# A hybrid decoder block on one core: the residual stream turned at wider steps, retention scores and the 1/rms spread placed later

## The chip, the cores and the metric

The kernel runs on one core of one Trainium2 chip. The metric is the time of one execution on the device in microseconds; the median of three runs of the kernel before is 2200.8 us (2198.17 to 2201.48). Engines are called by their names in the profile: PE multiplies matrices, ACT and DVE work on elements, SP issues the transfers, POOL does next to nothing here.

## What is computed

One decoder block, batch 1, 256 tokens, model width 2048, all in float32:

```python
h = x
h = h + 0.5 * swiglu(rms_norm(h, g1), w_gate1, w_up1, w_down1)        # d_ff 5632
n = rms_norm(h, g_mix)
rq, rk, rv, rg, sq, sk, sv = split(n @ w_in)
ret = retention(rope(rq), rope(rk), rv)       # 8 heads of 128, chunks of 128 tokens
#   s = (q k^T / sqrt(dk)) * decay mask, per head and chunk; intra = s v; state carried from chunk 0 to 1
ret = silu(rg) * group_norm(ret)
swa = sliding_window_attention(rope(sq), rope(sk), sv, sinks)
h = h + concat(ret, swa) @ w_out
h = h + memory_cross_attention(rms_norm(h), rms_norm(mem))
h = h + 0.5 * swiglu(rms_norm(h, g2), w_gate2, w_up2, w_down2)
return rms_norm(h, g_final)
```

## The kernel before

**Products.** Every float32 factor is split in two halves, a high one (a copy to the matmul format) and a low one (what that copy left out), and every product is three matmuls (L470, L471, L472): high by high, low weight by high, high weight by low. The weights are streamed. The unit of the stream is called a step: one piece of 128 x 1024 weights, which ACT copies to `wh` (L71), DVE subtracts to `wl` (L76), and PE uses in twelve matmuls of 128 x 512. A load (L203, 1 MB, on SP's queue) brings two steps. There are three load buffers `wf`, four buffers each of `wh` and `wl`; the halves are made three steps ahead of their matmuls.

**Turning.** Activations are made in one layout (tokens or features across the 128 partitions) and needed in the other. `cross` (L434 to L460) turns one tile pair: two DVE transposes of 32 x 32 blocks into two `t2k` tiles (L444), one step later two writes of 256 KB to a DRAM `box` (L449), two steps later eight reads of 64 KB back (L456), five steps after the start the caller's continuation, which copies or splits what came. All of this goes through the same SP queue as the weight loads, and SP's instructions run in the order in which the program was written.

**Order.** `later(n, task)` puts a task n steps on; `run_due` runs due tasks at the step boundaries between the matmuls. A task's instructions are ordered behind the ones already written on PE, ACT and DVE, so the delay numbers set the place of each task on all engines. PSUM has four temporary tiles `tmp` for such tasks and two accumulators `acc`; `t2k` has ten tiles.

**The three places.**
- The second feed-forward (FFN2) goes through pairs of gate and up units. A pair is 16 steps: eight of gate, after which ACT applies Silu (L507), and eight of up, after which DVE multiplies (L514) and `cross` turns the product. `begin_ffn2` also makes the four 512-column tiles of `h` be turned to the layout of the output (`turn_h`), which the down product at the end of FFN2 needs; this is a `cross` per tile, due 6, 10, 14 and 18 steps on.
- `rqk_done` turns and rotates a group of four retention heads' q and k (DVE L729 to L733) into `qk`; `ret_scores` then makes, per head, two matmuls into one `tmp` tile (L742, L743) and two masked DVE multiplications out of it (L746, L747). There are two groups, g = 0 and g = 1; the scores are due 2 and 3 steps on.
- `Norm.spread` makes 1/rms, which stands per token down the partitions, into rows along the free axis: two DVE broadcasts (L417), two PE transposes (L418), one copy to `rows`. `spread_over` (L425) reads it some 70 us later.

Of the kernel before, what the change touches and what calls it, by code (L numbers as in the profile page):

```python
# [11 lines left out]
F32 = mybir.dt.float32  # L12
F32R = mybir.dt.float32r
AF = mybir.ActivationFunctionType
ALU = mybir.AluOpType
AX = mybir.AxisListType

P = 128
S = 256
# [20 lines left out]
def decoder_block(ctx: ExitStack, tc: tile.TileContext, a: dict, out: bass.AP):  # L40
    nc = tc.nc
# [3 lines left out]
    work = ctx.enter_context(tc.tile_pool(name="work", bufs=1))  # L45
# [7 lines left out]
    def nm(s):  # L53
        uid[0] += 1
        return f"{s}_{uid[0]}"

    def blk(dt=F32R):

        return work.tile([P, 4, 2, S], dt, tag="blk", name=nm("blk"), bufs=13)

    def t2k(dt=F32):
        return work.tile([P, 512], dt, tag="t2k", name=nm("t2k"), bufs=10)

    def tmp_ps(dt=F32):
        return ps_tmp.tile([P, 512], dt, tag="tmp", name=nm("tmp"))
# [4 lines left out]
    def copy(dst, src, **kw):  # L70
        return nc.scalar.activation(dst, src, AF.Copy, **kw)  # L71
# [8 lines left out]
    ident = const.tile([P, P], F32, tag="ident", name="ident")  # L80
# [10 lines left out]
    ones = const.tile([P, P], F32, tag="ones", name="ones")  # L91
# [13 lines left out]
    def later(delay, fn):  # L105
        tasks.append((clock[0] + delay, len(tasks), fn))
# [251 lines left out]
    class Norm:  # L358
# [52 lines left out]

        def spread(self):

            tp = tmp_ps()
            for t in range(2):
                rep = t2k()[:, :P]
                nc.vector.tensor_scalar(rep, ones, self.rs[:, t : t + 1], None, ALU.mult)  # L417
                nc.tensor.transpose(tp[:, t * P : (t + 1) * P], rep, ident)  # L418
            self.rows = work.tile([P, S], F32, tag="rows", name=nm("rows"), bufs=1)
            copy(self.rows, tp[:, :S])  # L420

        def scale(self, t):
            return self.rs[:, t : t + 1]
# [7 lines left out]
    def squares_of(x):  # L431
        return x if len(x.shape) == 4 else x.rearrange("p (q g j) -> p q g j", q=4, g=4)

    def cross(src, then, room=None, delay=TURN):  # L434

        room = [None, None] if room is None else room
        boxes = []  # L440
        out = []
        sq = [t2k() for _ in src]
        for x, v in zip(sq, src):
            nc.vector.transpose(x.rearrange("p (g q j) -> p q g j", g=4, q=4), squares_of(v))  # L444

        def write():
            for x in sq:
                boxes.append(dram.tile([P, 512], F32, tag="box", name=nm("box")))
                nc.sync.dma_start(boxes[-1], x)  # L449

        def read():
            for box, dst in zip(boxes, room):
                dst = t2k() if dst is None else dst
                far = box.rearrange("(i r) (g n) -> g r i n", i=4, g=4)
                for g in range(4):
                    nc.sync.dma_start(dst[32 * g : 32 * g + 32, :].rearrange("p (i n) -> p i n", i=4), far[g])  # L456
                out.append(dst.rearrange("p (i q j) -> p q i j", i=4, q=4))
        later(1, write)
        later(2, read)
        later(delay, lambda: then(out))  # L460
# [252 lines left out]
    def rqk_done(g, which):  # L713
        def done(acc):
            def finish(out):
                if "rot" not in st:
                    st["rot"] = ctab[:, C_COSR : C_COSR + 512].rearrange("p (c s) -> p c s", c=2)
                    nmix.spread_over(st["rot"])
                if which == 0:
                    st["qk"] = blk(F32)  # L720
                qk = st["qk"]
                for t in range(2):
                    x = out[t]
                    cos, sin = (
                        st["rot"][:, c, t * P : (t + 1) * P].rearrange("p (o a j) -> p o a j", o=1, a=4)
                        .broadcast_to([P, 4, 4, 32]) for c in range(2)
                    )
                    r = squares_of(t2k())
                    nc.vector.tensor_tensor(r[:64], x[64:], sin[64:], ALU.mult)  # L729
                    nc.vector.tensor_tensor(r[64:], x[:64], sin[:64], ALU.mult)  # L730
                    nc.vector.tensor_tensor(x, x, cos, ALU.mult)
                    dst = qk[:, :, which, t * P : (t + 1) * P].rearrange("p q (a j) -> p q a j", a=4)
                    nc.vector.tensor_tensor(dst, x, r, ALU.add)  # L733
                if which == 1:
                    for i in range(4):
                        later(2 + i // 2, lambda i=i: ret_scores(g, i, qk))
            cross([acc[:, t, :] for t in range(2)], finish)
        return done

    def ret_scores(g, i, qk):  # L740
        ps = tmp_ps()
        nc.tensor.matmul(ps[:, :S], qk[:, i, 1, :P], qk[:, i, 0, :], start=True, stop=True)  # L742
        nc.tensor.matmul(ps[:, S : S + P], qk[:, i, 1, P:], qk[:, i, 0, P:], start=True, stop=True)  # L743
        sT = t2k()
        dm = st["dmat"][:, g * 4 + i, :]
        nc.vector.tensor_tensor(sT[:, :S], ps[:, :S], dm, ALU.mult)  # L746
        nc.vector.tensor_tensor(sT[:, S : S + P], ps[:, S : S + P], dm[:, :P], ALU.mult)  # L747
        st["sT", g, i] = sT
# [181 lines left out]

    n2 = Norm(G_FFN2, "n2", 4)
    to_h(a["xa_wo"], xo, 1.0, range(4), n2, lambda b: begin_ffn2(b))
    units[-3].then, units[-4].then = None, units[-3]

# [7 lines left out]
    def turn_h(b):  # L942
        if b == 0:
            h.extend(blk(F32).rearrange("p k c s -> p (k c s)") for _ in range(2))

        def made(out):
            for t in range(2):
                copy(squares_of(h[t][:, b * 512 : (b + 1) * 512]), out[t])
        cross([hT[b][:, :, t * P : (t + 1) * P].rearrange("p q (a j) -> p q a j", a=4) for t in range(2)], made)
# [52 lines left out]
    def begin_ffn2(b):  # L1002
        if b == 3:
            for b in range(4):
                later(6 + 4 * b, lambda b=b: turn_h(b))

    ffn(n2, a["ffn2_w_gate"], a["ffn2_w_up"], ffn2_down)
    run_stream()
# [83 lines left out]
```

## Time and profile before

| | before |
|---|---|
| median of three runs | 2200.8 us |
| profiled execution, its own time | 2198.31 us |
| span of its trace | 2196.5 us |
| PE busy | 2175.0 us (99%) |
| DVE busy | 1291.7 us (59%) |
| ACT busy | 1027.5 us (47%) |
| mean granted PE clock | 0.998 |
| moved by DMA | 472.04 MB, 215 GB/s |

The profile comes from one execution. The time of that execution is 1.8 us longer than its span, and 2.5 us under the median. PE is the engine that sets the time; a difference can only come from the moments in which PE waits or runs at a lower clock, and these are few. So the rows to look for are PE's waits, the stretches in which PE's busy time falls short, and what the engine named as releaser was doing itself.

### The profile page before, as it was taken

Reading aid. Unit: us, or ns where it says so; the run is one execution under the profiler, and the core shown is the slowest. Engines: PE = TensorE matmul, PEld = TensorE weight load, DVE = VectorE, ACT = ScalarE, POOL = GpSimd, SP = SyncE. Lnnn points to the kernel's source line nnn. Section 1 sums busy time; section 2 is a strip of 40 time slices with the busy share of each in tenths; the row PEclk is TensorE's granted clock in tenths of the full one; section 3 lists DMA queues with packets and bytes.
Section 4 is the critical chain, followed back from the end, with each engine's and each line's share of the span. In section 5 each row is a group of like instructions: output and inputs, shape, how many; then the busy total and the mean of one; then the engine's idle time right before and its main releaser. Section 6 shows DMA issues by size and latency. Waiting matters only on the chain.

```text
span 2196.5 us, 25627 instructions
## 1 busy us (share of the span) xinstructions
PE 2175.0 (99%) x9844; PEld 1804.2 (82%) x9844; DVE 1291.7 (59%) x1536; ACT 1027.5 (47%) x1258; POOL 10.4 (0%) x17
## 2 busy tenths in 40 slices
PE   9999999999999999999999999999899999999998
PEld 7888888888888888888888888887788888888886
DVE  6555555455556778886775555575555544555554
ACT  6444444444445554544564544454444433444443
POOL 0000000000000000000000000000000000000000
PEclk9999999999999999999999999999999999999999
DMA  7766677667667555556867654676766655666663
GB/s 269 233 217 211 216 228 232 215 214 234 206 222 262 201 185 191 174 191 207 270 232 245 215 174 171 210 250 214 246 214 215 226 196 195 215 207 220 216 215 144
DMA packets 187451, 472.04 MB, mean 215 GB/s; under 512 B 15552, under 2 KB 71616, under 8 KB 187200
## 3 DMA queue, kind: packets, MB, share of 16 engines
q1 hardware_dynamic: 187040, 470.22, 63.7%
q8 instruction: 77, 1.26, 0.2%
q14 instruction: 46, 0.38, 0.1%
q10 hardware_dynamic: 288, 0.18, 0.0%
HBM read 439.93 MB, written 30.41 MB: 214 GB/s over the span
## 4 chain that ended last, share of the span: by engine, by line
PE 95%; DVE 2%; DMA 1%; issue 1%; ACT 0%; SPq 0%; ACTq 0%; POOLq 0%; POOL 0%; DVEq 0%
PE acc L471 31%; PE acc L472 31%; PE acc L470 31%; DMA wf<-in_ffn_w_up 1%; DVE wl L76 1%; PE tmp L471 0%; PE tmp L472 0%; PE tmp L470 0%; ACT wh L71 0%; PE tmp L646 0%; DMA t2k<-box 0%; PE tmp L620 0%; DVE t2k L730 0%; DVE t2k L444 0%; PE tmp L742 0%
## 5 line engine op out<-in xcount | busy, mean ns | idle before, releaser
L76 DVE TENSOR_TENSOR wl<-wf,wh 128x1024 fp32r<-128x1024 f32 (+1 forms) x776 | 942.8, 1217 | 810.0 <-ACT wh L71 803.0
L71 ACT ACTIVATE wh<-wf 128x1024 fp32r<-128x1024 f32 (+1 forms) x776 | 817.4, 1056 | 1014.1 <-PE acc L472 955.9
L470 PE MATMUL acc<-wh,blk 128*128 128x512 f32 (+1 forms) x3104 | 1208.1, 389 | 4.4 <-ACT wh L71 3.2
L471 PE MATMUL acc<-wl,blk 128*128 128x512 f32 (+1 forms) x3104 | 1206.4, 389 | 4.7 <-DVE wl L76 4.6
L472 PE MATMUL acc<-wh,blk 128*128 128x512 f32 (+1 forms) x3104 | 1205.9, 388 | 0.0
L471 PEld LDWEIGHTS acc<-wl,blk 128*128 128x128 f32 x3104 | 583.3, 188 | 125.4 <-DVE wl L76 6.8
L470 PEld LDWEIGHTS acc<-wh,blk 128*128 128x128 f32 x3104 | 583.3, 188 | 124.4 <-ACT wh L71 3.6
L472 PEld LDWEIGHTS acc<-wh,blk 128*128 128x128 f32 x3104 | 583.1, 188 | 120.7 <-DVE blk L356 0.4
L444 DVE STREAM_TRANSPOSE t2k<-t2k 128x512 f32<-128x512 f32 x76 | 49.4, 687 | 16.8 <-ACT t2k L71 16.8
L71 ACT ACTIVATE blk<-t2k 128x512 fp32r<-128x512 f32 (+2 forms) x74 | 44.8, 608 | 9.2 <-DMA t2k<-box 7.3
L76 DVE TENSOR_TENSOR blk<-t2k,blk 128x512 fp32r<-128x512 f32 (+1 forms) x66 | 44.2, 672 | 0.0
L507 ACT ACTIVATE t2k<-acc,n 128x512 f32<-128x512 f32 x44 | 27.9, 686 | 31.6 <-PE acc L472 31.5
L514 DVE SCALAR_TENSOR_TENSOR t2k<-acc,n,t2k 128x512 f32<-128x512 f32 x44 | 31.0, 746 | 15.6 <-PE acc L472 15.6
L71 ACT ACTIVATE blk<-tmp 128x512 fp32r<-128x512 f32 (+2 forms) x53 | 23.9, 459 | 27.5 <-DVE blk L76 19.0
L71 ACT ACTIVATE blk<-h,gains 128x256 fp32r<-128x256 f32 x64 | 27.3, 496 | 5.7 <-DVE h L481 5.7
L356 DVE SCALAR_TENSOR_TENSOR blk<-h,gains,blk 128x256 fp32r<-128x256 f32 x64 | 26.9, 479 | 1.7 <-ACT blk L71 1.7
L393 DVE TENSOR_TENSOR t2k<-t2k,t2k 128x512 f32<-128x512 f32 x35 | 24.0, 685 | 2.3 <-ACT t2k L389 1.0
L76 DVE TENSOR_TENSOR blk<-tmp,blk 64x256 fp32r<-64x256 f32 (+2 forms) x45 | 22.2, 494 | 4.8 <-ACT blk L71 4.5
L471 PE MATMUL tmp<-blk,blk 128*128 128x256 f32 (+1 forms) x80 | 22.6, 282 | 0.6 <-DVE blk L76 0.6
L472 PE MATMUL tmp<-blk,blk 128*128 128x256 f32 (+1 forms) x80 | 22.5, 282 | 0.0
L470 PE MATMUL tmp<-blk,blk 128*128 128x256 f32 (+1 forms) x80 | 22.5, 281 | 0.0
L481 DVE TENSOR_TENSOR h<-h,t2k 128x512 f32<-128x512 f32 x32 | 21.0, 684 | 0.0
(122 smaller groups left out, 433.0 us busy)
## 6 DMA issues: line engine op xcount, KB each, us to landing
wf<-in_ffn_w_down SPq DMA_DIRECT2D x88, 1024.0 KB, 4.9
wf<-in_ffn_w_gate SPq DMA_DIRECT2D x87, 1024.0 KB, 5.1
wf<-in_ffn_w_up SPq DMA_DIRECT2D x87, 1024.0 KB, 5.2
box<-t2k SPq DMA_DIRECT2D x108, 256.0 KB, 2.1
t2k<-box SPq DMA_DIRECT2D x432, 64.0 KB, 4.7
wf<-in_w_in_rqk SPq DMA_DIRECT2D x16, 1024.0 KB, 5.1
wf<-in_w_in_rvg SPq DMA_DIRECT2D x16, 1024.0 KB, 5.0
wf<-in_w_out SPq DMA_DIRECT2D x16, 1024.0 KB, 5.1
```

Of the source, the lines that this page charges most:

```text
L71: return nc.scalar.activation(dst, src, AF.Copy, **kw)
L76: nc.vector.tensor_tensor(lo, src, hi, ALU.subtract)
L356: nc.vector.scalar_tensor_tensor(x[:, k, 1, :], v[:, k, :], g, x[:, k, 0, :], ALU.mult, ALU.subtract)
L393: nc.vector.tensor_tensor(self.sums, self.sums, y, ALU.add)
L444: nc.vector.transpose(x.rearrange("p (g q j) -> p q g j", g=4, q=4), squares_of(v))
L470: nc.tensor.matmul(o, ah, bh, start=start, stop=False)
L471: nc.tensor.matmul(o, ah, bl, start=False, stop=False)
L472: nc.tensor.matmul(o, al, bh, start=False, stop=stop)
L481: nc.vector.tensor_tensor(v, v, out[t], ALU.add)
L507: nc.scalar.activation(gated[b][t], acc[:, t, :], AF.Silu, scale=norm.scale(t))
L514: nc.vector.scalar_tensor_tensor(s[t], acc[:, t, :], norm.scale(t), s[t], ALU.mult, ALU.mult)
```

## The change

Three edits, with no instruction added or left out on PE, DVE, ACT or SP:

1. `begin_ffn2`: the four turnings of `h` are due 19, 35, 51 and 67 steps on instead of 6, 10, 14 and 18.
2. `rqk_done`: the four score tasks are due 4, 4, 5, 5 steps on instead of 2, 2, 3, 3.
3. `Norm.spread`: the two DVE broadcasts go into one `t2k` tile; the PE transposes and the copy are a task of their own, due two steps later.

```diff
         def spread(self):
 
-            tp = tmp_ps()
+            rep = t2k()[:, :S]
             for t in range(2):
-                rep = t2k()[:, :P]
-                nc.vector.tensor_scalar(rep, ones, self.rs[:, t : t + 1], None, ALU.mult)
-                nc.tensor.transpose(tp[:, t * P : (t + 1) * P], rep, ident)
-            self.rows = work.tile([P, S], F32, tag="rows", name=nm("rows"), bufs=1)
-            copy(self.rows, tp[:, :S])
+                nc.vector.tensor_scalar(rep[:, t * P : (t + 1) * P], ones, self.rs[:, t : t + 1], None, ALU.mult)
+
+            def turned():
+                tp = tmp_ps()
+                for t in range(2):
+                    ts = slice(t * P, (t + 1) * P)
+                    nc.tensor.transpose(tp[:, ts], rep[:, ts], ident)
+                self.rows = work.tile([P, S], F32, tag="rows", name=nm("rows"), bufs=1)
+                copy(self.rows, tp[:, :S])
+            later(2, turned)
...
-                        later(2 + i // 2, lambda i=i: ret_scores(g, i, qk))
+                        later(4 + i // 2, lambda i=i: ret_scores(g, i, qk))
...
-                later(6 + 4 * b, lambda b=b: turn_h(b))
+                later(19 + 16 * b, lambda b=b: turn_h(b))
```

The changed kernel's lines from L431 on are five higher (L444 becomes L449, L742 becomes L747).

**SP's queue at the second turning, early in FFN2, before.** `t2k_11644` and `t2k_11645` are the transposed tile of `h`, `t2k_11668` and `t2k_11669` the product of the up unit:

```order
L203 DMA wf_11652<-in_ffn_w_gate 128x2x1024
L449 DMA box_11672<-t2k_11644 128x512
L449 DMA box_11674<-t2k_11645 128x512
L456 DMA t2k_11695<-box_11672 32x4x128 x4
L456 DMA t2k_11700<-box_11674 32x4x128 x4
L449 DMA box_11705<-t2k_11668 128x512
L449 DMA box_11707<-t2k_11669 128x512
L203 DMA wf_11713<-in_ffn_w_up 128x2x1024
L456 DMA t2k_11624<-box_11705 32x4x128 x4
L456 DMA t2k_11625<-box_11707 32x4x128 x4
L203 DMA wf_11759<-in_ffn_w_up 128x2x1024
```

The turning of `h` stands directly ahead of the turning of the product, with one weight load between the two groups of reads and one behind them.

**The same queue in the changed kernel, at the first turning.** `t2k_11807` and `t2k_11808` are the transposed tile of `h`, `t2k_11966` that of the product:

```order
L203 DMA wf_11787<-in_ffn_w_up 128x2x1024
L454 DMA box_11828<-t2k_11807 128x512
L454 DMA box_11830<-t2k_11808 128x512
L203 DMA wf_11836<-in_ffn_w_gate 128x2x1024
L461 DMA t2k_11850<-box_11828 32x4x128 x4
L461 DMA t2k_11855<-box_11830 32x4x128 x4
L203 DMA wf_11880<-in_ffn_w_gate 128x2x1024
L203 DMA wf_11916<-in_ffn_w_gate 128x2x1024
L203 DMA wf_11950<-in_ffn_w_gate 128x2x1024
L454 DMA box_11987<-t2k_11966 128x512
```

Each of the four turnings now stands in this place, four weight loads away from the turning of the product, in a pair of units of its own.

**PE at the first scores of group 0, before.** `blk_6172` holds the rotated q and k:

```order
L470 MATMUL acc_6252<-wh_6380,blk_5377 128x512
L471 MATMUL acc_6252<-wl_6381,blk_5377 128x512
L742 MATMUL tmp_6474<-blk_6172 128x256
L472 MATMUL acc_6252<-wh_6380,blk_5377 128x512
L470 MATMUL acc_6534<-wh_6406,blk_4713 128x512
```

**PE at the same scores in the changed kernel:**

```order
L476 MATMUL acc_6509<-wl_6406,blk_4713 128x512
L477 MATMUL acc_6509<-wh_6405,blk_4713 128x512
L747 MATMUL tmp_6522<-blk_6171 128x256
L748 MATMUL tmp_6522<-blk_6171 128x128
L747 MATMUL tmp_6528<-blk_6171 128x256
L748 MATMUL tmp_6528<-blk_6171 128x128
L475 MATMUL acc_6509<-wh_6434,blk_4713 128x512
```

The first score matmul has moved behind thirteen more matmuls of the stream, and the scores stand in two groups of two heads at step boundaries.

**PE at the spread of 1/rms, before:**

```order
L470 MATMUL acc_5346<-wh_5451,blk_5377 128x512
L418 MATMUL tmp_5536<-ident,t2k_5537 128x128
L471 MATMUL acc_5346<-wl_5452,blk_5377 128x512
L418 MATMUL tmp_5536<-ident,t2k_5540 128x128
L472 MATMUL acc_5346<-wh_5451,blk_5377 128x512
```

**PE at the spread in the changed kernel:**

```order
L475 MATMUL acc_5585<-wh_5467,blk_4713 128x512
L476 MATMUL acc_5585<-wl_5468,blk_4713 128x512
L477 MATMUL acc_5585<-wh_5467,blk_4713 128x512
L422 MATMUL tmp_5598<-ident,t2k_5536 128x128 x2
L475 MATMUL acc_5585<-wh_5520,blk_4713 128x512
```

The two transposes stand together behind seventeen more matmuls of the stream.

## Rows read from the trace of the kernel before

**Rows 1.** The page, part 1: engine, busy us, share, instructions.

```profile
PE 2175.0 (99%) x9844; PEld 1804.2 (82%) x9844; DVE 1291.7 (59%) x1536; ACT 1027.5 (47%) x1258; POOL 10.4 (0%) x17
```

**Rows 2.** PE's waits, whole span: us in total, times, longest.

```profile
PE acc L471 <- DVE wl L76: 4.6, 3, 3.6
PE acc L470 <- ACT wh L71: 3.2, 1, 3.2
```

**Rows 3.** Windows: stretch, busy us (x instructions) by engine, granted clock, DMA share, GB/s.

```profile
100.00:700.00 600.00, 600.00 (x2649) 496.82 (x2648) 325.75 (x313) 265.72 (x283) 0.00 (x0) 1.00 0.67 223
...
1540.00:1550.00 10.00, 9.55 (x35) 7.73 (x36) 3.90 (x4) 3.36 (x5) 0.00 (x0) 0.83 0.63 216
```

**Rows 4.** DVE's timeline, four ends of up units: start, us, instruction, [idle before].

```profile
1503.37 1.41 DVE L514 SCALAR_TENSOR_TENSOR t2k<-acc,n,t2k 128x512 f32<-128x512 f32 x2
...
1553.05 1.41 DVE L514 SCALAR_TENSOR_TENSOR t2k<-acc,n,t2k 128x512 f32<-128x512 f32 x2 [7.96 <-PE acc L472]
...
1600.46 1.41 DVE L514 SCALAR_TENSOR_TENSOR t2k<-acc,n,t2k 128x512 f32<-128x512 f32 x2 [0.40 <-PE acc L472]
...
1643.98 1.41 DVE L514 SCALAR_TENSOR_TENSOR t2k<-acc,n,t2k 128x512 f32<-128x512 f32 x2 [0.40 <-PE acc L472]
```

**Rows 5.** PE's timeline, the two long waits among the turnings.

```profile
1539.19 0.50 PE L470 MATMUL acc<-wh,blk 128*128 128x512 f32 x1 [3.15 <-ACT wh L71]
...
1556.83 0.50 PE L471 MATMUL acc<-wl,blk 128*128 128x512 f32 x1 [3.58 <-DVE wl L76]
```

**Rows 6.** SP's queue ahead of the first long wait: issue start, time of the issues.

```profile
1522.49 0.87 SPq L449 DMA_DIRECT2D box<-t2k  x2
1528.73 3.96 SPq L456 DMA_DIRECT2D t2k<-box  x8
1532.79 0.91 SPq L203 DMA_DIRECT2D wf<-in_ffn_w_up  x2
```

**Rows 7.** ACT's waits from 1505 to 1556 us.

```profile
ACT wh L71 <- DMA wf<-in_ffn_w_up: 11.3, 3, 4.5
```

**Rows 8.** SP's queue in a later pair of units, where no `h` is turned.

```profile
1602.51 0.94 SPq L449 DMA_DIRECT2D box<-t2k  x2
...
1604.65 5.36 SPq L456 DMA_DIRECT2D t2k<-box  x8
1610.11 0.40 SPq L203 DMA_DIRECT2D wf<-in_ffn_w_up  x1
...
1630.00 0.37 SPq L203 DMA_DIRECT2D wf<-in_ffn_w_gate  x1
```

**Rows 9.** ACT's timeline in the same pair: Silu, and the copy of a later step.

```profile
1622.22 1.27 ACT L507 ACTIVATE t2k<-acc,n 128x512 f32<-128x512 f32 x2 [1.66 <-PE acc L472]
...
1641.26 1.06 ACT L71 ACTIVATE wh<-wf 128x1024 fp32r<-128x1024 f32 x1 [1.66 <-PE acc L472]
```

**Rows 10.** DVE's timeline in the same pair, behind Silu.

```profile
1624.46 1.23 DVE L76 TENSOR_TENSOR wl<-wf,wh 128x1024 fp32r<-128x1024 f32 x1 [2.65 <-ACT wh L71]
```

**Rows 11.** The page, part 6: transfers, number, KB each, median us to landing.

```profile
wf<-in_ffn_w_gate SPq DMA_DIRECT2D x87, 1024.0 KB, 5.1
...
box<-t2k SPq DMA_DIRECT2D x108, 256.0 KB, 2.1
t2k<-box SPq DMA_DIRECT2D x432, 64.0 KB, 4.7
```

**Rows 12.** PE's timeline at the spread and at the scores of both groups.

```profile
761.09 0.33 PE L418 MATMUL tmp<-ident,t2k 128*128 128x128 f32 x1 [0.53 <-DVE t2k L417]
...
862.02 0.67 PE L742 MATMUL tmp<-blk 128*128 128x256 f32 x2 [0.68 <-DVE blk L733]
...
965.70 0.67 PE L742 MATMUL tmp<-blk 128*128 128x256 f32 x2 [0.71 <-DVE blk L76]
```

**Rows 13.** DVE's timeline at the spread and at the scores of group 0.

```profile
761.09 0.28 DVE L417 TENSOR_SCALAR t2k<-ones,nmix 128x128 f32<-128x128 f32 x1
...
863.90 0.68 DVE L733 TENSOR_TENSOR blk<-t2k,t2k 128x512 f32<-128x512 f32 x1
```

## The prediction

> **What bounds the kernel now.** I read part 1 of the page first. PE is busy for 2175.0 of the 2196.5 us of the span [rows 1], so all that any change of order can win lies in the 21.5 us in which PE is idle, and in moments of a lower clock. The windows give the pace: from 100 to 700 us PE does 2649 matmuls in 600 us without a gap [rows 3], 0.2265 us each, and a step of twelve takes 2.72 us. PE's waits then say where the gaps are: 4.6 us for the low half of a weight (DVE) and 3.2 us for the high half (ACT) [rows 2]; both long ones lie between 1535 and 1557 us [rows 5], early in FFN2, where the turnings of `h` stand now. Three waits of 0.5 to 0.7 us lie at the spread and at the scores [rows 12]. The weight halves themselves are late there only because ACT waits 11.3 us for weight loads [rows 7], and SP's queue shows why: 256 KB writes and 64 KB reads of the turnings hold the queue, and a pair of loads that ACT needs is issued only at 1532.79, behind eight reads that themselves had to wait until 1528.73 [rows 6]. So in that stretch the last thing to come is a weight load, held up by other entries of its own queue.
>
> **Turnings, what goes away.** The price is read from a clock that the kernel carries itself: the end of each up unit on DVE. In an undisturbed pair of units it comes after 1643.98 - 1600.46 = 43.52 us [rows 4], which is the 16 steps of 2.72. From 1503.37 to 1600.46 there are two pairs, 97.09 us instead of 87.04, so **10.05 us** are lost there. The waits of rows 2 account for 7.8 of them (4.6 + 3.2); the other 2.2 are matmuls that run slower after the first long wait (the granted clock is 0.83 from 1540 to 1550 [rows 3], so part of that window is at 1.2 instead of 2.4 GHz) and slow restarts.
>
> **Turnings, what is put in their place.** The same eight instructions on SP and two on DVE now come once in each of four pairs of units, just behind Silu. I walk through it with the pair around 1622 us, in which nothing is turned there. DVE: Silu starts at 1622.22 [rows 9], and DVE is idle for 2.65 us before its next subtraction at 1624.46 [rows 10]. The two transposes take 1.3 us, worked out from the product's turning: its write is issued at 1602.51, 2.05 us behind the start of an L514 pair that lasts 1.41 [rows 4, 8], so the first transpose takes 0.64 at most. They fall into that hole, or push the subtraction by a few tenths, which three steps of halves in store cover. SP: the two writes are issued by about 1625.5, land 2.1 us later [rows 11], and the eight reads start near 1627.5. They hold the queue as long as the product's own reads do, 5.36 us [rows 8], the longest such row, against 3.96 for eight in rows 6; so to 1633 at the latest. The load behind them was issued at 1630.00 before [rows 8] and goes out 3 us later; it lands 5.1 us on [rows 11], at 1638.1, and ACT opens it at 1641.26 [rows 9]. That leaves about **3 us in hand**. The same thing already happens in each pair at the product's own turning: reads from 1604.65, the next load only at 1610.11, and PE has no gap [rows 3, 8]. ACT's copies of what was read come from reads that land 4.7 us after issue [rows 11]; they find idle time of 1.66 us before each weight copy [rows 9]. So I put the four turnings in their new places at nothing. The bounds are 0 and what the two long waits cost now, 5.0 us per turning (10.05 / 2); I take 0, since the product's turning is the nearest row by far, and the cover is the 3 us above: if the load is later than that, PE pays the excess once per pair. The last turning is due at step 67 from the start of FFN2's stream, long before the down product at its end, so nothing new waits for `h`.
>
> A rule of the Trainium skill speaks against this edit. The page DMA: Bandwidth & Descriptors, section Rules for kernel authors, says to issue a DMA early, compute, and wait for it late, so that its fixed cost overlaps; a turning that is put off for up to 49 steps goes the other way. By that rule this term would be 0 instead of 10.05. The trace does not agree for this queue, since the early reads and writes there are just what holds up the loads [rows 6, 7]. The rule's case is priced among the rivals.
>
> **Scores.** Each of the two waits at L742 lasts 0.68 and 0.71 us [rows 12]; a wait costs PE 0.16 more than its idle time, because a matmul row lasts 0.39 us in the steady run and the next starts after 0.23. That makes 0.84 + 0.87 = 1.71 us. Of the first, the cause is DVE's rotation: the second half of q and k is ready at 863.90 + 0.68 = 864.58 [rows 13]. In the new order thirteen matmuls of the stream, 2.9 us, come between the old and the new place, and PE had been ready for the old one at 861.18: 862.02 - 0.84 = 861.18 and 2.9 make 864.1, or up to 1 us later, since small matmuls of the sliding-window attention that followed the score now stand ahead of it. So the wait there lies between 0 and 0.5 us; I take 0.2 at most and count none. The second wait was for a `tmp` tile that DVE had not emptied; two steps (5.44 us) later DVE has done so. DVE's masked multiplications come later by as much, and the products that read them stay where they are, one to three steps behind; by the order of DVE's work I estimate one to two us of margin there. Bounds of the term: -1.7 to +1.7, as each of the four places where someone waits for DVE could show one such wait; taken: **1.7 gained**.
>
> **Spread.** The wait of 0.53 us [rows 12] costs 0.69. The second broadcast starts at 761.09 and takes 0.28 us [rows 13]. PE comes to the moved transposes seventeen matmuls later, 3.9 us, so not before 764. Nothing waits there. The copy to `rows` is read 70 us later. Bounds 0 to 0.7, taken **0.7 gained**.
>
> **Sum.** 10.05 + 1.7 + 0.7 = 12.45 us. The profiled execution (2198.31 us, of which 2196.5 is the span) would go to 2185.9, with a span near 2184.0. It lay 2.5 us under the median, so against the median of 2200.8 the forecast is 2188.3; I write **2188**. What is left of idle time on PE is the start of the kernel, one wait in the sliding-window part, and the ends.
>
> **Rivals.**
> - *A held load is late in every pair.* The 3 us in hand are used up because writes, reads and loads land later when they overlap. For it: eight 64 KB reads hold the queue for anything from 3.96 to 5.36 us [rows 6, 8]. Against: the product's turning is covered. If PE waits a quarter of today's price per turning, 4 x 1.26 = 5.0 us come back: 2193.3. Chance 0.14.
> - *It is not the spacing.* The turnings cost their 10.05 us in total wherever they stand, because the queue has to carry 32 small reads in any case: 2200.8 - 2.4 = 2198.4. For it: the reads alone hold SP for 4 to 5 us each time [rows 6, 8]. Against: the later pair carries one such group without loss [rows 4]. The rule of the Trainium skill quoted above gives this time, and so does the advice in the same section to merge transfers under 64 KB: by both of them, spacing is no cure. Chance 0.09.
> - *Slower.* Each turning alone makes a long wait of its own: a load that comes late empties the three steps of halves, and PE then drops to the lower clock, as it did once [rows 3, 5]. At 5.0 us each, four make 20.1 instead of 10.05: 2200.8 - 2.4 + 10.05 = 2208.4. It decides against the change from 3.1 us per turning on (12.45 / 4). It needs the load to be late by 6 us where I see 3 us in hand. Chance 0.05.
> - *The scores only move their wait*, both times, by the nearest price, 0.85 each: 2190.0. Chance 0.04.
>
> **How the numbers follow.** Forecast 0.68, and the rivals 0.14, 0.09, 0.05 and 0.04. About 0.2%, 4.4 us, is what a measurement of this kernel can tell from no change. Below 2196.4 lie the forecast, the last rival and nearly all of the first: 0.85 faster. Within 0.2% lie the second and the edge of the first: 0.10. Above lies the slower rival: 0.05. The range starts 4 us under the forecast, since the runs shown spread over 3.3 us, and reaches over the first rival to 2196, leaving out the second and the third.
>
> **What would show it.** In the profile of the changed kernel: no row of PE waiting for `wh` or `wl` for over 0.3 us between 1495 and 1700 us, 43.5 us between the ends of all up units of FFN2, a granted clock of 1.00 in every window there; no row at L747 or L422 among PE's waits, or one of up to 0.3 us. The load behind the turning's reads would be issued about 3 us behind its time, and ACT would still wait for PE, not for it. A wait of ACT for a gate load, once per pair, would mean the first or third rival; waits that keep their size with the reads apart, the second. Wrong altogether would be a new wait elsewhere, for instance at the products that read the scores.

## The result

The changed kernel takes 2185.02 us (median of four runs, 2184.3 to 2185.41); the kernel before takes 2200.99 us (four runs, 2198.17 to 2201.48). The ratio is 0.993, with a 95% interval of 0.9912 to 0.9947: faster by 16.0 us. The forecast was 2188, the range 2184 to 2196. The direction is right and the time lies in the range, 1 us above its lower end, but 3.3 us more were gained than the sum of 12.45 and the median of then (2200.8) gave, and the experiments below show that one part of the explanation was wrong.

### The profile page after: what moved, and what is told of

It reads as the page before. It is cut to its first block, busy times and chain, and to the rows that moved or that the text cites. A ratio compares the mean times of both kernels' runs of the same rounds, so it can differ in the third digit from the quotient of the medians.

```text
span 2182.5 us, 25627 instructions
## 1 busy us (share of the span) xinstructions
PE 2171.4 (99%) x9844; PEld 1804.0 (83%) x9844; DVE 1292.2 (59%) x1536; ACT 1027.1 (47%) x1258; POOL 9.5 (0%) x17
## 4 chain that ended last, share of the span: by engine, by line
PE 99%; DVE 0%; issue 0%; DMA 0%; ACT 0%; SPq 0%; ACTq 0%; POOLq 0%; POOL 0%
PE acc L475 32%; PE acc L476 32%; PE acc L477 32%; PE tmp L476 0%; PE tmp L477 0%; PE tmp L475 0%; DMA wf<-in_ffn_w_gate 0%; PE tmp L651 0%; PE tmp L625 0%; PE tmp L747 0%; PE tmp L404 0%; PE tmp L701 0%; PE tmp L769 0%; PE tmp L768 0%; PE tmp L766 0%
## 5 line engine op out<-in xcount | busy, mean ns | idle before, releaser
L449 DVE STREAM_TRANSPOSE t2k<-t2k 128x512 f32<-128x512 f32 x76 | 49.4, 687 | 16.8 <-ACT t2k L71 16.8
```

## The profile after

The profiled execution took 2184.3 us, with a span of 2182.5. The first fence is the page's head and part 1, then all of PE's waits (us in total, times, longest).

```profile
span 2182.5 us, 25627 instructions
...
PE 2171.4 (99%) x9844; PEld 1804.0 (83%) x9844; DVE 1292.2 (59%) x1536; ACT 1027.1 (47%) x1258; POOL 9.5 (0%) x17
```

```profile
PE tmp L95 <- POOL ident masks.py:199: 1.4, 1, 1.4
PE acc L475 <- ACT blk L71: 0.7, 1, 0.7
PE tmp L476 <- DVE blk L76: 0.6, 1, 0.6
```

The two rows that answer to [rows 2] are gone, and so are those of the scores and the spread [rows 12]. What stays is the start and one wait in the sliding-window part. The windows over the stretch in which the turnings stood (columns as in [rows 3]) have no idle time on PE and the upper clock level throughout:

```profile
1530.00:1540.00 10.00, 10.00 (x46) 8.28 (x45) 4.90 (x4) 4.69 (x6) 0.00 (x0) 1.00 0.75 235
1540.00:1550.00 10.00, 10.00 (x46) 8.29 (x45) 6.64 (x8) 4.25 (x4) 0.00 (x0) 1.00 0.65 219
1550.00:1560.00 10.00, 10.00 (x45) 8.28 (x45) 5.73 (x6) 5.02 (x6) 0.00 (x0) 1.00 0.74 220
```

To see where the 14.0 us between the two profiled spans came from, I cut each span at two places that every variant of this kernel has: the column sums on PE (L404) of FFN1's norm and those of FFN2's. Their rows in PE's timeline, of the kernel before and then of the changed one:

```profile
46.74 0.61 PE L404 MATMUL tmp<-ones,t2k 128*128 128x1 f32 x4
...
1484.59 0.60 PE L404 MATMUL tmp<-ones,t2k 128*128 128x1 f32 x4
```

```profile
45.90 0.61 PE L404 MATMUL tmp<-ones,t2k 128*128 128x1 f32 x4
...
1481.01 0.61 PE L404 MATMUL tmp<-ones,t2k 128*128 128x1 f32 x4
```

So the start takes 46.7 and 45.9 us, the middle (with the spread and the scores) 1437.85 and 1435.11, and the tail (FFN2 with the turnings, to the end of the span) 711.91 and 701.49. The tail gave 10.4 us, the middle 2.7, and 0.8 is the start, which the change does not touch.

At one of the new places of a turning, SP's queue after the change (start, time of the issues), and ACT's copy of the step that the load behind the reads serves:

```profile
1565.01 0.94 SPq L454 DMA_DIRECT2D box<-t2k  x2
1568.26 0.38 SPq L203 DMA_DIRECT2D wf<-in_ffn_w_gate  x1
1568.74 5.35 SPq L461 DMA_DIRECT2D t2k<-box  x8
1574.25 9.55 SPq L203 DMA_DIRECT2D wf<-in_ffn_w_gate  x3
```

```profile
1564.76 1.27 ACT L512 ACTIVATE t2k<-acc,n 128x512 f32<-128x512 f32 x2 [1.66 <-PE acc L477]
...
1583.80 1.06 ACT L71 ACTIVATE wh<-wf 128x1024 fp32r<-128x1024 f32 x1 [1.66 <-PE acc L477]
```

In [rows 8, 9] that load went out 7.78 us behind the start of Silu, here 9.49 us: 1.7 us later, where 3 had been forecast, and some 4.5 us ahead of its use with the 5.0 us that a gate load takes to land in this stretch. ACT waits for PE, not for the load.

## The experiments

All times below are medians, each beside runs of the kernel before on the same chip (medians from 2200.28 to 2200.76). The table gives the three stretches of the profiled execution of each run.

| kernel | time, us | ratio (95%) | start | middle | tail |
|---|---|---|---|---|---|
| before | 2200.99 | | 46.7 | 1437.85 | 711.9 |
| changed | 2185.02 | 0.993 (0.9912 to 0.9947) | 45.9 | 1435.11 | 701.5 |
| turn_only | 2188.50 | 0.9943 (0.9929 to 0.9958) | 48.7 | 1437.80 | 701.5 |
| scores_only | 2197.55 | 0.9989 (0.998 to 0.9999) | 45.8 | 1435.63 | 713.2 |
| spread_only | 2201.34 | 1.0 (0.999 to 1.0009) | 47.1 | 1437.00 | 715.9 |
| before_again | 2200.43 | 0.9998 (0.9988 to 1.0007) | 47.3 | 1437.78 | 712.1 |
| sixteen_from6 | 2188.27 | 0.9944 (0.9928 to 0.9961) | 46.2 | 1437.86 | 701.5 |
| four_from19 | 2188.70 | 0.9944 (0.9929 to 0.9959) | 47.3 | 1437.82 | 701.8 |
| eight_from19 | 2188.43 | 0.9944 (0.9929 to 0.9958) | 47.3 | 1437.80 | 701.6 |
| sixteen_from11 | 2189.50 | 0.9948 (0.9933 to 0.9963) | 47.4 | 1437.80 | 701.9 |
| pool_queue | 2194.58 | 0.997 (0.9958 to 0.9982) | 46.5 | 1437.77 | 708.9 |
| reads_later | 2190.64 | 0.9951 (0.9934 to 0.9967) | 48.7 | 1437.86 | 702.4 |
| reads_16 | 2186.18 | 0.9933 (0.9918 to 0.9947) | 47.6 | 1434.88 | 701.6 |
| reads_32 | 2204.67 | 1.0015 (1.0005 to 1.0025) | 48.6 | 1435.24 | 722.1 |

### Each edit alone

The first three kernels are the kernel before with one edit of the change each, the fourth is the kernel before itself.

```diff
 # turn_only
-                later(6 + 4 * b, lambda b=b: turn_h(b))
+                later(19 + 16 * b, lambda b=b: turn_h(b))
 # scores_only
-                        later(2 + i // 2, lambda i=i: ret_scores(g, i, qk))
+                        later(4 + i // 2, lambda i=i: ret_scores(g, i, qk))
 # spread_only: the new spread, whose transposes and copy become a task
+            later(2, turned)
```

> Only the four turnings of h are put 16 steps apart, from step 19 on. Theory (a weight load was late behind other entries of SP's queue, and one turning per pair of units is covered): from the column-sum matmuls ahead of FFN2 (L404, 1484.59 us in the kernel before) to the end 701.5 us instead of 711.9, so 10.4 us less; no PE wait between 1490 and 1700 us. The waits at the scores and at the spread stay as they were. Time about 2190 us. Rival (part of the 14 us between the two profiled runs comes from an effect of the other two edits on FFN2): less than 9 us gained here.

Measured: tail 701.51, so 10.4 us gained in the trace, 12.3 by the medians. All of the tail's gain is the turnings'.

> Only the score tasks are two steps later. Theory: PE's two waits at L742 go, 1.7 to 1.9 us, and the turnings keep their 10 us; time about 2199 us, which the medians alone can hardly tell from 2201. Rival (the wait only moves): a PE wait of 0.5 us or more stays at L742 or comes up at the products that read the scores.

Measured: the middle is 2.2 us shorter, and no wait at L742 is left; the time falls by 3.2 us between medians, 2.4 by the ratio. The rival is out. How much cover there is shows in the changed kernel's timelines. DVE's first half of k ends at 859.61 + 0.69 = 860.30; the first score (L747) reads only that half of k and starts at 863.04. The second half ends at 862.32 + 0.69 = 863.01; the matmul that reads it is L748, whose weight load starts at 863.26, 0.25 us later.

```profile
859.61 0.69 DVE L738 TENSOR_TENSOR blk<-t2k,t2k 128x512 f32<-128x512 f32 x1
...
862.32 0.69 DVE L738 TENSOR_TENSOR blk<-t2k,t2k 128x512 f32<-128x512 f32 x1
```

```profile
863.04 0.59 PE L747 MATMUL tmp<-blk 128*128 128x256 f32 x2
```

```profile
863.26 0.40 PEld L748 LDWEIGHTS tmp<-blk 128*128 128x128 f32 x2
```

> Only the spread of 1/rms is cut into two tasks. Theory: PE's wait of 0.53 us at the transposes goes, 0.7 us; the other waits stay. Rival: no wait goes, since DVE is as late at the new place.

Measured: the wait is gone and the middle is 0.85 us shorter. The medians cannot tell that, but the middle can: in the nine profiles with the old spread and the old scores it lies between 1437.77 and 1437.86. The tail of this kernel's profiled execution is 4 us longer than that of the profile before, so its whole time does not show the gain.

> The kernel before once more, for what its executions have in spread: two of them took 2198.2 us and three 2200.8 to 2201.5. Theory A: the long waits among the turnings differ from execution to execution (L404 to the end 711.9 us in the profiled one, 714 to 715 us in a slow one). Theory B: the start differs (up to L404 1484.6 us in the profiled one, 1486 to 1488 in a slow one).

Both theories hold in part. Over the kernels that keep the old turnings, the tail is 711.9, 712.1, 713.2 and 715.9 us; over all profiles, the start goes from 45.8 to 48.7. In this run's own profile (2199.01 us, below its median) neither is far from the profile before, so no execution of the kernel before at its median or above was profiled. The tail of the eight kernels without a long PE wait in it lies between 701.5 and 702.4. So in these profiles the tail varies only where PE stalls. PE's waits behind the 715.9 (spread_only):

```profile
PE acc L476 <- DVE wl L76: 5.6, 4, 3.6
PE acc L475 <- ACT wh L71: 2.6, 1, 2.6
```

They count two more short waits than the profile before has from 700 us on (4.3 us in two there), and the matmuls behind each of the two long waits run at the lower clock for a while, where in the first profile only those behind the first one did. Against the waits of the first profile (4.3 + 3.2 us) that is 0.7 us more; the other 3.3 of the 4.0 lie in slower matmuls and restarts: from 1540 to 1565 us three stretches of 5 us have a granted clock of 0.50, 0.84 and 0.66, in the first profile one has 0.66.

### Distance or place

The edit sets two numbers at once, the first step and the distance. Four kernels take them apart; each is the kernel before with only this line changed:

```diff
-                later(6 + 4 * b, lambda b=b: turn_h(b))
+                later(6 + 16 * b, lambda b=b: turn_h(b))     # sixteen_from6
+                later(19 + 4 * b, lambda b=b: turn_h(b))     # four_from19
+                later(19 + 8 * b, lambda b=b: turn_h(b))     # eight_from19
+                later(11 + 16 * b, lambda b=b: turn_h(b))    # sixteen_from11
```

> The kernel before with the turnings of h due 6 + 16 b steps on: the old first place, the new distance. Theory (it is the crowding of four turnings and the product's own in one queue): each turning now stands five steps ahead of the product's own, in a pair of units of its own, and nearly all of the 10.4 us is gained; L404 to the end 701.5 to 703 us. Rival (it is the place in the pair, behind Silu, that counts): a wait of 1 us or more in each of the four pairs, 706 to 712 us.

> The kernel before with the turnings due 19 + 4 b steps on: the new first place, the old distance. Theory (crowding): the four turnings and one product's turning again share 16 steps of the queue, and 5 to 12 us are lost there; L404 to the end 706 to 713 us. Rival (the old start was bad because FFN2 had just begun and its stream was not yet full): 702 us.

> The kernel before with the turnings due 19 + 8 b steps on: the first and third behind Silu, the second and fourth together with the product's own turning. Theory: the first and third cost nothing; the second and fourth put 16 reads in a row into the queue, so that the load behind them is late by 8 us or so where 4 are in hand and three steps (8 us) of halves are in store: 0 to 4 us lost at each, L404 to the end 702 to 708 us. Rival (only four steps apart is too close): 701.5 us.

> The kernel before with the turnings due 11 + 16 b steps on: 16 steps apart, but each together with the product's own turning, so 16 reads in a row. Theory (the queue is what counts, not the distance as such): the next load goes out some 8 us late where about 4 us are in hand, ACT waits for it in each of the four pairs, and PE waits once the three steps of halves in store (8 us) are used up: 0 to 4 us a pair, L404 to the end 702 to 718 us, with ACT waits on loads in any case. Rival (only the distance counts): no ACT wait on loads, 701.5 us.

All four gain what turn_only gains. The second is a miss of my theory: four turnings and one of the product again share 16 steps, four steps apart, and PE loses at most 0.3 us. Its rival had the number, 702 us, but its reason, that FFN2 has just begun, does not carry alone, since sixteen_from6 starts there too. The first shows that the old place alone is no harm either. Of the kernels so far, only those with both the old place and the small distance stall PE. The theories of the last two (702 us and more) missed as well: no ACT wait on a load came in either. In sixteen_from11 that is so although 16 reads hold the queue for 9.3 us, so more time was in hand there than I had counted.

What the old place and the small distance each do shows in the waits of SP's queue from 1480 to 1700 us (us in total, times, longest), of the kernel before, sixteen_from6, four_from19 and the changed kernel in this order:

```profile
SPq L456 <- DMA box<-t2k: 30.2, 6, 7.8
```

```profile
SPq L456 <- DMA box<-t2k: 27.9, 8, 5.2
```

```profile
SPq L456 <- DMA box<-t2k: 5.2, 4, 2.0
```

```profile
SPq L461 <- DMA box<-t2k: 0.6, 1, 0.6
```

In the old places SP stands still at the reads until the writes have landed. (In the same view SP also stands at the reads for 9.0, 13.6, 17.1 and 17.1 us that the profile puts down to weight loads; that part is longest where nothing stalls.) SP's rows of the kernel before show it at the first turning: a weight load, the two writes right behind it, and the reads only at 1495.96, 6.2 us after the first write.

```profile
1489.13 0.37 SPq L203 DMA_DIRECT2D wf<-in_ffn_w_gate  x1
1489.76 0.94 SPq L449 DMA_DIRECT2D box<-t2k  x2
1495.96 4.69 SPq L456 DMA_DIRECT2D t2k<-box  x8
1500.75 0.91 SPq L203 DMA_DIRECT2D wf<-in_ffn_w_gate  x2
```

The next loads stand behind that wait. The same view, 1485 to 1565 us, gives the median time to landing of a write as 6.4 us before and 2.7 us after (the last number of each row):

```profile
box<-t2k SPq DMA_DIRECT2D x12, 256.0 KB, 6.4
```

```profile
box<-t2k SPq DMA_DIRECT2D x6, 256.0 KB, 2.7
```

Taken pair by pair in the kernel before, the two writes of 1514.66, which stand behind reads, land in 2.3 us; those right behind a load (1489.76, 1522.49, 1558.36) in 6.2 to 6.4, and those behind two loads issued in one go (1501.75, 1533.79) in 9.2 and 8.5.

In the new place the writes come 3 us ahead of a load, in the old one 0.6 us behind one, and the load that would keep the engines fed stands ahead of the reads in the new order and behind them in the old. A turning in the old place thus takes SP some 5 us more, once per pair without harm (ACT then waits 6.3 us for gate loads between 1480 and 1720 us in sixteen_from6, all of it covered by the halves in store); in four_from19 the crowding alone costs ACT 12.7 us of waits on loads, covered as well; both together cost 17.5 us, and PE stalls. Of ACT's waits on loads, 1480 to 1720 us, first sixteen_from6, then four_from19:

```profile
ACT wh L71 <- DMA wf<-in_ffn_w_gate: 6.3, 3, 2.2
```

```profile
ACT wh L71 <- DMA wf<-in_ffn_w_up: 10.2, 3, 5.9
...
ACT wh L71 <- DMA wf<-in_ffn_w_gate: 2.5, 2, 2.0
```

Waits on loads are not all of it. ACT makes the halves and the copies of what was read in one order, and in the kernel before it also stands at those copies, besides the 11.3 us of [rows 7]:

```profile
ACT blk L71 <- DMA t2k<-box: 7.1, 6, 2.1
...
ACT wh L71 <- DMA wf<-in_ffn_w_gate: 6.2, 3, 3.3
ACT wh L71 <- DMA t2k<-box: 1.7, 1, 1.7
```

All of ACT's waits that a transfer ended, in this window, come to 26.3 us there and to 21.0 to 26.0 in the three other profiles with the old turnings, all of which stall. They come to 8.0 us in sixteen_from6, 13.9 in four_from19 and at most 2.2 in the changed kernel, turn_only, eight_from19 and sixteen_from11.

### Is it the queue, and is it that wait

Two kernels keep the old places. One gives the h turnings to POOL's queue, the other puts the reads two steps later, with a load ahead of most of them.

```diff
 # pool_queue, in cross, for turn_h alone
-                nc.sync.dma_start(boxes[-1], x)
+                queue.dma_start(boxes[-1], x)                # queue=nc.gpsimd; the reads likewise
 # reads_later, in cross, for turn_h alone (delay=TURN + 2, back=4)
-        later(2, read)
+        later(back, read)
```

> The kernel before, with the writes and reads of the h turnings issued by POOL instead of SP, at the old places, four steps apart. Theory (weight loads are late because they stand behind other entries of SP's queue): the long PE waits go, L404 to the end 701.5 to 704 us. Rival (the transfers themselves, their bytes and small pieces, crowd out the weight loads whatever queue issues them): 709 us or more.

Neither number came: the tail is 708.9, between the two. The waits on weight loads are gone from ACT, as the theory wants, but POOL's reads land late (6.2 us by the median), and ACT, whose instructions also run in order, stands at the copies of what was read. ACT's waits that a transfer ended come to 22.0 us, all of them at those copies. Its timeline shows two such waits (the second one put down to a write) and the weight copies that queue up behind the second; PE then waits 3.4 us once and drops to the lower clock. POOL's writes land late too, 5.8 us by the median, though no load stands in their own queue.

```profile
1518.39 0.63 ACT L71 ACTIVATE blk<-t2k 128x512 f32<-128x512 f32 x1 [6.44 <-DMA t2k<-box]
...
1533.52 0.63 ACT L71 ACTIVATE blk<-t2k 128x512 f32<-128x512 f32 x1 [6.50 <-DMA box<-t2k]
...
1534.94 3.88 ACT L71 ACTIVATE wh<-wf 128x1024 fp32r<-128x1024 f32 x4
```

So this run moves the stall from one in-order queue to another; it doesn't decide between queue and transfers by itself.

> The kernel before, the turnings of h at their old places (6 + 4 b), but the reads of each come four steps behind its transposes instead of two, and the copies two steps later, so that a weight load stands between the writes and the reads. Theory (in the old places the writes stand right behind a 1 MB load and land late, 6.4 us instead of 2.7 by the median; SP waits for them at the reads, 30 us in all, and the next load stands behind that wait): SP's wait for the writes falls under 10 us, PE has no long wait, L404 to the end 701.5 to 703 us, although the turnings stay four steps apart. Rival (four turnings in 16 steps are too many in any case where FFN2 begins): PE waits of 2 us or more remain, 706 us or more.

Measured: SP's wait for the writes falls from 30.2 to 16.0 us, less far than expected, and PE's long waits are gone; one of 0.55 us is left, and the tail is 702.35. The distance and the first step are the old ones, and the writes land as slowly as before (6.4 us by the median), so neither the crowding nor the late landing by itself stalls PE.

```profile
SPq L456 <- DMA box<-t2k: 16.0, 6, 4.6
```

The load that PE's first long wait hangs on, the third of the up unit, shows what the later reads do. In the kernel before it goes out at 1532.79, behind the reads that waited for their writes [rows 6], 48.2 us behind L404 of FFN2; ACT, which has waited 3.09 us for it, opens it at 1538.09:

```profile
1538.09 2.00 ACT L71 ACTIVATE wh<-wf 128x1024 fp32r<-128x1024 f32 x2 [3.09 <-DMA wf<-in_ffn_w_up]
```

In reads_later it stands ahead of the reads:

```profile
1522.95 1.04 SPq L449 DMA_DIRECT2D box<-t2k  x2
1524.09 0.65 SPq L203 DMA_DIRECT2D wf<-in_ffn_w_up  x1
1529.21 5.72 SPq L456 DMA_DIRECT2D t2k<-box  x8
```

```profile
1534.72 2.01 ACT L71 ACTIVATE wh<-wf 128x1024 fp32r<-128x1024 f32 x2 [4.06 <-DMA wf<-in_ffn_w_up]
```

Counted from L404 (at 1486.55 in reads_later), it goes out 10.7 us earlier, and ACT opens it 5.3 us earlier, more than PE's first wait of 3.15. So SP standing at the reads with that load behind it made the first long wait. ACT's waits on loads as such hardly fall, from 17.5 to 16.1 us:

```profile
ACT wh L71 <- DMA wf<-in_ffn_w_up: 10.8, 3, 4.2
...
ACT wh L71 <- DMA wf<-in_ffn_w_gate: 5.3, 3, 2.5
```

What is gone are its waits at the copies, which come two steps later in this kernel too. How much of the gain that part makes was not tried apart.

### How much the new place bears

The changed kernel, with every read of an h turning cut in two (32 KB, sixteen of them) or four (16 KB, thirty-two):

```diff
-                    nc.sync.dma_start(dst[32 * g : 32 * g + 32, :].rearrange("p (i n) -> p i n", i=4), far[g])
+                    at = dst[32 * g : 32 * g + 32, :].rearrange("p (i n) -> p i n", i=4)
+                    for c in range(0, 4, 4 // cuts):
+                        nc.sync.dma_start(at[:, c : c + 4 // cuts, :], far[g][:, c : c + 4 // cuts, :])
```

> The changed kernel with the eight reads of each h turning cut into sixteen of 32 KB. Theory: they hold SP's queue for about 10 us instead of 5.4, the gate load behind them goes out 5 us later than in the changed kernel (there it had about 4 us in hand), ACT waits for it about 1 us once per pair, and PE does not wait, since three steps of halves are in store; time as the changed kernel. Rival (a transfer's cost goes by its bytes): the queue is held as before, and ACT has no wait.

> The changed kernel with the eight reads of each h turning cut into thirty-two of 16 KB. Theory: they hold SP's queue for 20 us, the load behind them is 15 us later than in the changed kernel; with 4 us in hand and 8 us in store PE waits 3 us or more in each of the four pairs, at the lower clock afterwards: 12 to 25 us slower than the changed kernel. This is the slower rival of the prediction made on purpose. Rival: bytes alone count, no loss.

SP's rows of a turning, first with sixteen reads, then with thirty-two:

```profile
1570.18 9.02 SPq L463 DMA_DIRECT2D t2k<-box  x16
1579.30 5.93 SPq L203 DMA_DIRECT2D wf<-in_ffn_w_gate  x3
```

```profile
1575.25 17.85 SPq L463 DMA_DIRECT2D t2k<-box  x32
1593.20 1.42 SPq L203 DMA_DIRECT2D wf<-in_ffn_w_gate  x3
```

Sixteen reads hold the queue for 9.0 us and put the load 3.6 us later than in the changed kernel (13.1 instead of 9.5 us behind Silu); ACT has not the 1 us of waiting that I expected, and the tail stays at 701.6. Thirty-two hold it for 17.9 us, and PE loses 20.6 us (722.1 against 701.5): PE's waits there, and ACT's on gate loads, show the chain that the prediction's slower rival describes. ACT also stands 26.0 us at the copies of the late pieces, which that rival did not name.

```profile
PE acc L477 <- ACT wh L71: 8.7, 3, 3.4
PE acc L478 <- DVE wl L76: 2.7, 4, 0.8
```

```profile
ACT wh L71 <- DMA wf<-in_ffn_w_gate: 16.1, 9, 3.2
```

## Why the prediction came out as it did

**Size of the turnings' term.** 10.05 us were read from the ends of the up units [rows 4]; the tail gave 10.4 in the profiled executions, and turn_only alone as much. The missing 0.4 lies in the first of the four ends: DVE came late to it, with no idle time before it, and in the changed kernel too the first pair takes 43.11 us and the later ones 43.52. Reading the loss from the kernel's own clock rather than from the waits alone was right. The waits among the turnings are 7.5 of it (4.3 + 3.2), not 7.8: one of the three in the first line of [rows 2], 0.3 us, lies ahead of 700 us.

**The step that was off: from the profiled execution to the median.** The prediction put the 2.5 us between the profiled execution and the median of before on top of the changed kernel's time as well. In the changed kernel it is 0.7 us (2185.02 against 2184.3). The gap is no property of the runs as such: part of it came, as far as the profiles tell, from the very stalls that the change removes. Where they stand, the tail varies from 711.9 to 715.9 us, and the profile that the forecast started from has the shortest; where they don't, it varies by 0.9. How much of the 2.5 us is the tail and how much the start is not shown, since no execution at the median was profiled. The times agree, though from few runs: 25 of the kernel before on one chip go from 2197.39 to 2204.42, four of the changed one from 2184.3 to 2185.41. Against the profile (2198.3), the forecast of 2185.9 missed the 2184.3 by 1.6: 0.8 is the start, which differs from execution to execution, 0.4 the turnings, and the rest the scores and the spread.

**Scores and spread.** The forecast was 1.7 + 0.7 = 2.4 us; alone they gave 2.2 and 0.85, together 2.7 (2.6 to 3.0 in the three profiles that have both). The waits that were to go are gone, as forecast. One reading was wrong: the old wait at the first score ended at 862.02, so it was for DVE's first half of k (861.19 + 0.69 = 861.88), not for the second, which is ready only at 864.58 [rows 13]. In the new order the second half bears on L748 alone, and there it is ready 0.25 us ahead; the 0 to 0.5 us that I feared did not come. DVE's row of the first half, before:

```profile
861.19 0.69 DVE L733 TENSOR_TENSOR blk<-t2k,t2k 128x512 f32<-128x512 f32 x1
```

**Why the stall was there.** Here the prediction was right in the large (a weight load late behind other entries of SP's queue) and wrong in the reason: it named the writes and reads themselves and their crowding. Crowding alone does not stall PE (four_from19), nor does the old place (sixteen_from6). What the row at 1528.73 in [rows 6] showed, 6.2 us after the writes at 1522.49, was SP waiting for a write to land; I counted the time and did not ask what it was waiting for. For the new places I took 2.1 us to landing from the median of the whole kernel [rows 11]; that the writes there do not stand right behind a load, as they do in the old places, was luck, though the distance alone would have been enough (sixteen_from6). I also left out ACT's waits at the copies of what was read. The rival that it is not the spacing is out, since spacing alone removes the loss; but spacing is not the only cure (four_from19, reads_later).

**The rule that speaks against the edit.** The prediction quoted the Trainium skill, DMA: Bandwidth & Descriptors, Rules for kernel authors: issue early, wait late. The runs side with neither time of issue, since early turnings 16 steps apart and late ones 4 apart cost nothing. To wait late is what reads_later does between a write and its reads, and there the loss falls from 10.4 to 0.9 us. What decided here was the second transfer of a chain: issued in order behind the first, it waits for it on the queue that also carries the loads.

**The margin.** 3 us in hand were forecast for the load behind the reads; the profile after shows about 4.5, and reads_16 used 3.6 of them without a wait. The slower rival needed the load to be late by 6 us; in reads_32, where the reads hold the queue for 17.9 us, it goes out 14.8 us later than in the changed kernel (24.25 us behind Silu), and that costs more than the whole change gains.

## What to carry to other kernels

Where a queue runs in order, look not only at how long its entries take but at what each waits for: a read of something just written makes everything behind it wait for the write, and here a write issued right behind a large load landed late. Put other useful entries between the write and the read, or leave the queue a stretch in which it can catch up; either was enough here (reads_later, sixteen_from6), though reads_later also moved the copies. Look as well at the engine that uses what is read: it too runs in order, and its waits add to those for the loads. And when a change removes stalls, carry over to the new time only the run-to-run spread that the stalls did not make.

## What the runs showed of the hardware

- A 256 KB write to DRAM took 2.7 us to land by the median in the changed kernel, where no load stood right ahead of it (1485 to 1565 us), and 6.4 us in the kernel before, where 1 MB loads mostly did: 2.3 us behind reads, 6.2 to 6.4 behind one load, 8.5 and 9.2 behind two.
- Small reads held SP by their number more than by their bytes: eight of 64 KB 5.35 us, sixteen of 32 KB 9.0 us, thirty-two of 16 KB 17.9 us. Each of these rows holds one wait of 1.7, 1.7 and 2.2 us that the profile puts down to a load; without it a read takes 0.46 to 0.49 us of SP, whatever its size.
- The first 46 to 49 us of the kernel, which are the same instructions in every variant, differ by up to 2.9 us between the profiled executions.
